# Leading products first in the block products and the down products, and the second block sum written over a weight block

## The chip, the cores and the metric

The kernel runs on one core of one Trainium2 chip. The metric is the device time of one execution in microseconds (us); the runs of the kernel before have a median of 2973.24 us (three runs, 2968.42 to 2973.53 us).

## The reference

What is computed is a decoder of two layers on 1024 tokens of width 1024, all in float32:

```python
for layer in range(DEPTH):                       # DEPTH = 2
    h = rmsnorm(x, norm_mix[layer])
    if layer < N_A_LAYERS:                       # layer 0: sparse attention, three gated branches
        mix = nsa_attention(h, a_w_in[i], ..., a_w_out[i], rel_bias)
    else:                                        # layer 1: shared keys and values, three dilated windows
        kv = (rmsnorm(x, kv_norm) @ kv_w).reshape(B, S, N_DIL, 2, N_KV, HEAD_DIM)
        mix = dilated_attention(h, b_w_q[j], k_shared, v_shared, b_w_out[j], rel_bias)
    x = x + mix
    x = x + swiglu(rmsnorm(x, norm_ffn[layer]), ffn_w_up[layer], ffn_w_down[layer])
return rmsnorm(x, final_norm)

def swiglu(h, w_up, w_down):
    a, b = jnp.split(h @ w_up, 2, axis=-1)       # w_up: 1024 x 5632, w_down: 2816 x 1024
    return (jax.nn.silu(a) * b) @ w_down
```

## The kernel before

**Products in three parts.** A float32 operand is split into a leading part h, rounded to the matmul's format on ScalarE (ACT), and a remainder l, a subtraction on VectorE (DVE). A product of two operands is then three matmuls: h by h, h by l, and l by h. `mm3` issues them in this order for one 128x128 piece of the stationary side, on its lines 203, 204 and 205. `Pairs` makes such a pair for a 128x512 operand: line 884 writes `ph` on ACT, line 885 writes `pl` on DVE (or, early in a stage, on GpSimd, POOL). There are five `ph` and five `pl` buffers, so a sixth pair waits until the first has been read by its last matmul.

**Block products.** The feed-forward up product, and the projection of keys, values and queries behind the first layer (`project_B`), are products of 2x2 blocks by the scheme of seven multiplications instead of eight. `cols_steps` does one block of 128 output columns: the weights come as four 128x512 blocks a11, a12, a21, a22 (`raw`, the tile names `oT` and `oTb` in the profile), and seven products m1 to m7 multiply a weight block, or a sum of blocks, by one of seven prepared operands of the token side, `B11`, `B21`, `B22` and `T1` to `T4`. `blk` issues a product: four pieces by three matmuls, 12 matmuls into one PSUM bank. POOL makes the sums: s1 = a21 + a22 (line 1112), a21 = a11 - a21 (line 1113), s2 = s1 - a11 (line 1127), a12 = a12 - s2 (line 1129). m5 multiplies s1 by T1, m6 multiplies s2 by T2, m7 a21 by T3, m4 a22 by T4, m3 a12 by B22. The banks: m1, m6, m7 and m4 accumulate in one bank after another (`ux`), which ACT copies out after m1 (line 1095), m6 (line 1134) and m7 (line 1143); m2 uses a bank that DVE empties on line 1104; m5 and m3 share one that DVE reads on lines 1144 and 1160.

**Down products.** Two hidden blocks of 128 columns make the operands of one call of `rows_steps`, again seven products of 12 matmuls: four row tiles t by three matmuls. Each row tile has a bank of its own, `dx0` to `dx3` for products that accumulate, `dr0` and `dr1` in turn for the others, and DVE adds a bank to the residual stream `xr` on line 943. Its sums run on POOL (lines 951 to 961).

**Order.** `staged` prepares a step (loads, sums, pairs) and then issues the matmuls of the step before. In `ffn`, two hidden blocks (14 block products) and the seven down products of the two blocks before are put in turn: two block products, one down product. A pair of hidden blocks is thus 252 matmuls. The order of a block's products is a string: in the feed-forward part "m1 m2 m5 m6 m7 m4 m3", in `project_B` "m1 m2 m6 m5 m7 m4 m3" for all but its first block. From these steps a scheduler works out, when the kernel is built, in which order each engine's instructions stand; on the chip each engine keeps that order. So matmuls of different steps are mixed where the scheduler took one to be ready before another.

**Loads.** Weight blocks of the feed-forward part turn through seven buffers (`wu`), those of `project_B` through ten; a load on SyncE's queue (SP) into a buffer waits for the last reader of what was in it. POOL multiplies each block by the norm's gains (lines 1269 and 1453). In the feed-forward part s2 is written over s1 (`s2=None`); in `project_B` it has a tile of its own.

Of the kernel before, what the change touches and what calls it, by code (L numbers as in the profile page):

```python
# [115 lines left out]
def trunk(ctx, tc, I, out):  # L116
    nc = tc.nc
# [83 lines left out]
    def mm3(ps, lhs, rhs, first, last, shared=False):  # L201
        (lh, ll), (rh, rl) = lhs, rhs
        nc.tensor.matmul(ps, lh, rh, start=first, stop=False, skip_group_check=bool(shared))  # L203
        nc.tensor.matmul(ps, lh, rl, start=False, stop=False, skip_group_check=bool(shared))  # L204
        return nc.tensor.matmul(ps, ll, rh, start=False, stop=last, skip_group_check=bool(shared))  # L205
# [189 lines left out]
    with ExitStack() as c:  # L395
# [145 lines left out]
        steps = compress(0, kc2, wts)  # L541
# [356 lines left out]
    def part(t, i):  # L898
        return t[0][:, i * 128:(i + 1) * 128], t[1][:, i * 128:(i + 1) * 128]
# [11 lines left out]
    def rows_steps(spare, pairs, tmp, blocks, xr):  # L911


        X, tA, tB = [], [], []
        n = len(blocks)

        def step(ops, onX, where, sums=None, whole=False, eng=(None, None)):
            def operands(i):
                if sums is not None:
                    sums(i, *blocks[i])  # L920
                return pairs(ops[0](i), eng[0]), pairs(ops[1](i), eng[1])

            def prep():
                ready = [operands(0)]

                def run():
                    if whole:
                        ready.extend(operands(i) for i in range(1, n))
                        order = [(i, t) for t in range(4) for i in range(n)]
                    else:  # L930
                        order = [(i, t) for i in range(n) for t in range(4)]
                    banks = X if onX else [bank(spare[t % len(spare)]) for t in range(4)]
                    if onX == 1:
                        X.extend(bank(f"dx{t}") for t in range(4))
                    for i, t in order:
                        if i == len(ready):
                            ready.append(operands(i))
                        a, b = ready[i]
                        mm3(banks[t], part(a, t), b, i == 0 and onX != 2, i == n - 1, onX)
                        if i == n - 1:  # L940
                            for r, c in where:
                                xs = xr[:, 4 * r + t, c * 512:(c + 1) * 512]
                                nc.vector.tensor_add(xs, xs, banks[t])  # L943
                return run
            return prep

        def sums1(i, a, b):
            (a11, a21, a12, a22), (b11, b12, b21, b22) = a, b
            tA.append(tmp("a", i))
            tB.append(tmp("b", i))  # L950
            nc.gpsimd.tensor_add(tA[i], a21, a22)
            nc.gpsimd.tensor_sub(tB[i], b12, b11)
            nc.gpsimd.tensor_sub(a21, a11, a21)
            nc.gpsimd.tensor_sub(b12, b22, b12)

        def sums2(i, a, b):
            (a11, a21, a12, a22), (b11, b12, b21, b22) = a, b
            nc.gpsimd.tensor_sub(tA[i], tA[i], a11)
            nc.gpsimd.tensor_sub(tB[i], b22, tB[i])
            nc.gpsimd.tensor_sub(a12, a12, tA[i])  # L960
            nc.gpsimd.tensor_sub(b21, b21, tB[i])

        P = nc.gpsimd if n > 1 else None
        A = lambda j: lambda i: blocks[i][0][j]
        B = lambda j: lambda i: blocks[i][1][j]
        T = lambda i: tA[i], lambda i: tB[i]
        return [step((A(0), B(0)), 1, [(0, 0)]),
                step((A(2), B(2)), 0, [(0, 0)]),
                step(T, 0, [(1, 1), (0, 1)], sums1),
                step(T, 2, [(0, 1)], sums2),  # L970
                step((A(2), B(3)), 0, [(0, 1)]),
                step((A(1), B(1)), 2, [(1, 1)], eng=(None, P)),
                step((A(3), B(2)), 2, [(1, 0)], whole=True, eng=(P, None))]
# [98 lines left out]
    def cols_steps(banks, order, pairs, tmp, ops, load, done, view=lambda x: x, eng=None):  # L1072
# [6 lines left out]
        held = lambda n, name: st.setdefault(n, bank(name)) if n not in st else st[n]  # L1079

        def blk(b, a, name, first, prev=None):
            for i in range(4):
                with after(prev if i == 0 else None):
                    mm = mm3(b, part(a, i), ops[name][i], first and i == 0, i == 3, True)
            return mm

        def m1():
# [34 lines left out]

        def m6():
            a11, a12, a21, a22 = st["W"]
            s = s1()
            s2 = tmp("s2") or s
            nc.gpsimd.tensor_sub(s2, s, a11)
            a = pairs(s2)
            nc.gpsimd.tensor_sub(a12, a12, s2)

            def run():
                blk(held("x", nx), a, "T2", False)
                st["d1"] = tmp("d1")
                nc.scalar.activation(st["d1"], view(st["x"][:]), AF.Copy)
            return run
# [116 lines left out]
    def ffn(p, scratch, B, xr, layer):  # L1252
# [1 line left out]
        pairs = Pairs(p, 5)  # L1254
        own = lambda n, bufs=1: p.tile([128, 512], F32, name=n, bufs=bufs)
        wu, ut = Turns(scratch[0:7]), Turns(scratch[7:13])
        misc = dict(c=scratch[13], s1=scratch[14], s2=None)
        wd = Turns([p.tile([128, 512], F32, name=f"wd{i}")[:] for i in range(3)] + scratch[15:])
        gains = g_ffn[layer]
        raw = {}  # L1260
# [19 lines left out]
        def hidden(j, u):  # L1280

            def ahead(f):
                if j == 1:
                    raw[2].clear()
                if 0 < j < NJ - 1:
                    for q in range(3):
                        load_up(j + 1, q)
                return f()

            def tmp(n):  # L1290
                if n in ("d0", "d1"):
                    return u[base + int(n[1])]
                return scratch[15] if (j, n) == (0, "c") else misc[n]

            def done(a, r, C):
                t = u[base + r]
                if a == 0:
                    nc.scalar.activation(t, C, AF.Silu)
                else:
                    nc.vector.tensor_mul(t, t, C)  # L1300

            base = 2 * (j % 2)
            banks = {0: ("dx2", "uy", "uy"), 1: ("dx3", "ux", "uy")}.get(j, ("ux", "uy", "uy"))
            steps = cols_steps(banks, "m1 m2 m5 m6 m7 m4 m3", pairs, tmp, B.ops, lambda: raw[j], done,
                               eng=nc.gpsimd if j < 3 else None)
            i = 2 if j in (1, 2) else 0
            steps[i] = steps[i][0], lambda f=steps[i][1]: ahead(f)

            def m4(f=steps[5][1]):
                if j == 0:  # L1310
                    raw[1].clear()
                if j + 1 < NJ:
                    for q in range(3 if j else 0, 4):
                        load_up(j + 1, q)
                return f()
            steps[5] = "m4", m4
            return steps
# [529 lines left out]
```

## Time and profile before

| | |
|---|---|
| median of the runs | 2973.24 us (2968.42 to 2973.53, three runs) |
| the profiled execution | 2975.66 us, its span 2973.8 us |
| mean granted TensorE clock | 0.989 |
| first attention stage | 0 to about 795 us |
| feed-forward part of layer 0 | about 795 to 1460 us |
| `project_B` | about 1460 to 1880 us |
| second attention stage | about 1880 to 2200 us |
| output projection and feed-forward part of layer 1 | about 2200 to 2960 us |

How to read the rows: PE is TensorE's matmuls, PEld its weight loads, DVE VectorE, ACT ScalarE, POOL GpSimd, SP SyncE. A name such as `ux<-T2h,ph` reads: into bank `ux`, moving operand the leading part of T2, stationary operand a `ph`. In the order of time, each row has the start, the duration, the engine, the line, the operation, and in brackets how long the engine sat idle before it and who released it. A matmul's duration there is longer than the distance to the next one, since matmuls overlap; so a short wait of the matmuls shows as a longer distance between two starts, and not in brackets.

### The profile page before, as it was taken

How to read it: one execution, taken by the hardware profiler on the slowest of the kernel's cores; microseconds unless marked ns; L12 is line 12 of the kernel's file. 1: busy time of each engine (PE TensorE's matmuls, PEld its weight loads, DVE VectorE, ACT ScalarE, POOL GpSimd, SP SyncE). 2: the span in 40 equal slices, each digit the busy share in tenths (PEclk: the TensorE clock that was granted, in tenths of full speed). 3: DMA queues.
4: the chain of work that ended last, by engine and by line, in shares of the span. 5: the costliest groups of instructions: out<-in, count | busy, mean ns of one | idle time of the engine just before them, and what ended most of it. 6: DMA issues, size and time to landing. Idle time of an engine off the chain costs nothing.

```text
span 2973.8 us, 44470 instructions
## 1 busy us (share of the span) xinstructions
PE 2842.3 (96%) x14734; PEld 2372.2 (80%) x14734; DVE 2394.0 (81%) x4866; ACT 1610.0 (54%) x3615; POOL 1616.4 (54%) x1727
## 2 busy tenths in 40 slices
PE   9999999999999999999999999899989999999997
PEld 8888888887777788788777788788867788887886
DVE  5543988988988888988875676699998888888887
ACT  5432988897553333333454444699965433333334
POOL 2135766764565555555456787444425755555552
PEclk9999999999999999999999999999999999999999
DMA  8678133113222222231224554865441211112112
GB/s 242 219 241 289 43 95 87 50 34 112 73 62 63 74 74 62 63 77 56 85 82 130 164 170 145 264 207 175 126 153 32 68 57 57 57 47 63 51 47 75
DMA packets 277318, 317.58 MB, mean 107 GB/s; under 512 B 19196, under 2 KB 210733, under 8 KB 277088
## 3 DMA queue, kind: packets, MB, share of 16 engines
q1 hardware_dynamic: 255344, 246.50, 28.0%
q0 software_dynamic: 21744, 68.23, 7.1%
q8 instruction: 117, 1.92, 0.3%
q14 instruction: 113, 0.93, 0.1%
HBM read 243.17 MB, written 87.20 MB: 111 GB/s over the span
## 4 chain that ended last, share of the span: by engine, by line
PE 60%; DVE 23%; ACT 6%; issue 4%; DMA 3%; POOL 3%; SPq 1%; DVEq 0%; POOLq 0%; ACTq 0%
PE ux L203 5%; DVE pl L885 5%; PE ux L204 5%; PE ux L205 5%; PE uy L203 4%; PE uy L204 4%; PE uy L205 4%; DVE xr L943 4%; PE dx L204 3%; PE dx L205 3%; PE pt L328 3%; PE dr L203 3%; PE dx L203 2%; PE mm L204 2%; PE dr L204 2%
## 5 line engine op out<-in xcount | busy, mean ns | idle before, releaser
L885 DVE TENSOR_TENSOR pl<-oT,ph 128x512 fp32r<-128x512 f32 x319 | 327.0, 1044 | 44.4 <-ACT ph L884 38.4
L884 ACT ACTIVATE ph<-oT 128x512 fp32r<-128x512 f32 x329 | 198.6, 625 | 208.6 <-PE ux L204 58.2
L328 PE MATMUL pt<-ident,P 128*128 128x128 f32 x1536 | 243.1, 276 | 11.2 <-DVE tl L166 5.1
L885 DVE TENSOR_TENSOR pl<-oTb,ph 128x512 fp32r<-128x512 f32 x233 | 219.5, 967 | 25.1 <-ACT ph L884 25.0
L166 DVE TENSOR_TENSOR tl<-pt,th 128x512 fp32r<-128x512 f32 (+1 forms) x336 | 217.6, 653 | 27.0 <-ACT th L165 25.6
L884 ACT ACTIVATE ph<-oTb 128x512 fp32r<-128x512 f32 x239 | 142.8, 625 | 168.6 <-PE ux L204 52.4
L943 DVE TENSOR_TENSOR xr<-xr,dr 128x512 f32<-128x512 f32 x320 | 204.4, 678 | 30.0 <-PE dr L205 30.0
L204 PE MATMUL dx<-pl,ph 128*128 128x512 f32 x512 | 205.8, 402 | 9.6 <-DVE pl L885 7.0
L165 ACT ACTIVATE th<-pt 128x512 fp32r<-128x512 f32 (+1 forms) x336 | 185.1, 564 | 40.2 <-PE pt L328 35.7
L803 POOL TENSOR_SCALAR P<-P,sm,gates 128x384 f32<-128x384 f32 (+7 forms) x256 | 182.4, 723 | 44.9 <-DVE sm L801 39.7
L328 PEld LDWEIGHTS pt<-ident,P 128*128 128x128 f32 x1536 | 178.4, 141 | 31.9 <-DVE tl L166 5.2
L943 DVE TENSOR_TENSOR xr<-xr,dx 128x512 f32<-128x512 f32 x320 | 200.0, 678 | 2.5 <-PE dx L205 1.8
L205 PE MATMUL dx<-ph,pl 128*128 128x512 f32 x512 | 201.4, 396 | 0.4 <-DVE pl L885 0.4
L203 PE MATMUL dx<-ph 128*128 128x512 f32 x512 | 164.6, 401 | 14.5 <-DVE nss L1016 7.9
L799 ACT ACTIVATE P<-P,m 128x384 f32<-128x384 f32 (+7 forms) x256 | 170.6, 669 | 9.2 <-DVE m L797 7.1
L1269 POOL TENSOR_TENSOR oT<-oT,gffn 128x512 f32<-128x512 f32 x92 | 108.8, 1188 | 121.9 <-DMA oT<-in_ffn_w_up_dram 98.5
L348 PE MATMUL o<-th,V 128*128 128x256 f32 x572 | 159.0, 297 | 5.1 <-POOL th L341 2.0
L349 PE MATMUL o<-tl,V 128*128 128x256 f32 x572 | 158.2, 299 | 3.2 <-DVE tl L166 1.5
L1269 POOL TENSOR_TENSOR oTb<-oTb,gffn 128x512 f32<-128x512 f32 x92 | 108.2, 1186 | 89.3 <-DMA oTb<-in_ffn_w_up_dram 74.4
L341 POOL TENSOR_SCALAR th<-traw 128x256 fp32r<-128x256 f32 x112 | 95.4, 852 | 101.9 <-ACT traw L340 37.1
L1646 ACT ACTIVATE P<-P,st 128x384 f32<-128x384 f32 (+2 forms) x256 | 139.8, 548 | 6.7 <-DVE st L1641 5.3
L203 PEld LDWEIGHTS dx<-ph 128*128 128x128 f32 x512 | 96.9, 190 | 43.9 <-ACT nss L1015 8.7
(631 smaller groups left out, 9502.6 us busy)
## 6 DMA issues: line engine op xcount, KB each, us to landing
qB<-xr POOLq DMA_DIRECT2D x96, 256.0 KB, 4.6
oT<-in_ffn_w_up_dram SPq DMA_DIRECT2D x92, 256.0 KB, 2.9
oTb<-in_ffn_w_up_dram SPq DMA_DIRECT2D x92, 256.0 KB, 3.0
Q<-qB SPq DMA_DIRECT2D x40, 512.0 KB, 5.9
wd<-in_ffn_w_down_dram SPq DMA_DIRECT2D x66, 256.0 KB, 2.6
oT<-in_b_w_q_dram SPq DMA_DIRECT2D x48, 256.0 KB, 4.2
K<-kBs SPq DMA_DIRECT2D x40, 256.0 KB, 9.9
wraw<-in_a_w_in_dram SPq DMA_DIRECT2D x18, 512.0 KB, 7.8
```

The source lines that it names most:

```text
L165: prev = nc.scalar.activation(H_, src, AF.Copy)
L166: rest = (eng or nc.vector).tensor_sub(L_, src, f32(H_))
L203: nc.tensor.matmul(ps, lh, rh, start=first, stop=False, skip_group_check=bool(shared))
L204: nc.tensor.matmul(ps, lh, rl, start=False, stop=False, skip_group_check=bool(shared))
L205: return nc.tensor.matmul(ps, ll, rh, start=False, stop=last, skip_group_check=bool(shared))
L328: nc.tensor.transpose(ps[:, i * 128:(i + 1) * 128], b, ident)
L799: nc.scalar.activation(P[:, e, :n], P[:, e, :n], AF.Exp, bias=mm[:, e:e + 1], scale=-1.0, accum_out=sm[:, e:e + 1])
L803: nc.gpsimd.tensor_scalar(P[:, e, :n], P[:, e, :n], sm[:, e:e + 1], gt(g, t, br, 2 * hp + e, 1), op0=OP.mult, op1=OP.mult)
L884: nc.scalar.activation(h, src, AF.Copy)
L885: (eng or nc.vector).tensor_sub(l, src, f32(h))
L943: nc.vector.tensor_add(xs, xs, banks[t])
L1269: nc.gpsimd.tensor_mul(v, v, gains[:, k:k + 4].unsqueeze(2).to_broadcast([128, 4, 128]))
```

## The change

Three things change. First, `blk` issues the twelve matmuls of a block product by kind: the four leading products (prepared h by weight h), then the four with the prepared operand's remainder, then the four with the weight pair's remainder `pl`. Second, `rows_steps` issues a down product by pairs of row tiles, 0 and 1, then 2 and 3, and within a pair by kind: leading, then the remainder of the left (stationary) operand, then that of the right one. Third, s2 is written over a11 and not over s1 or into a tile of its own, and the feed-forward part uses the order "m1 m2 m6 m5 m7 m4 m3" for all blocks but the first. The number of instructions on each engine stays as it is.

```diff
@@ rows_steps
...
-                    for i, t in order:
-                        if i == len(ready):
-                            ready.append(operands(i))
-                        a, b = ready[i]
-                        mm3(banks[t], part(a, t), b, i == 0 and onX != 2, i == n - 1, onX)
-                        if i == n - 1:
+                    (a, b), = ready
+                    for ts in ((0, 1), (2, 3)):
+                        for z, (u, v) in enumerate(((0, 0), (1, 0), (0, 1))):
+                            for t in ts:
+                                nc.tensor.matmul(banks[t], part(a, t)[u], b[v], start=z == 0 and onX != 2, stop=z == 2,
+                                                 skip_group_check=True)
+                        for t in ts:
                             for r, c in where:
                                 xs = xr[:, 4 * r + t, c * 512:(c + 1) * 512]
                                 nc.vector.tensor_add(xs, xs, banks[t])
@@ cols_steps, blk
-            for i in range(4):
-                with after(prev if i == 0 else None):
-                    mm = mm3(b, part(a, i), ops[name][i], first and i == 0, i == 3, True)
+            (ah, al), oh, ol = a, [o[0] for o in ops[name]], [o[1] for o in ops[name]]
+            for z, (x, ys) in enumerate(((ah, oh), (ah, ol), (al, oh))):
+                for i in range(4):
+                    with after(prev if (z, i) == (0, 0) else None):
+                        mm = nc.tensor.matmul(b, x[:, i * 128:(i + 1) * 128], ys[i], start=first and (z, i) == (0, 0),
+                                              stop=(z, i) == (2, 3), skip_group_check=True)
@@ cols_steps, m6
-            s = s1()
-            s2 = tmp("s2") or s
-            nc.gpsimd.tensor_sub(s2, s, a11)
-            a = pairs(s2)
-            nc.gpsimd.tensor_sub(a12, a12, s2)
+            nc.gpsimd.tensor_sub(a11, s1(), a11)
+            a = pairs(a11)
+            nc.gpsimd.tensor_sub(a12, a12, a11)
@@ ffn
-            steps = cols_steps(banks, "m1 m2 m5 m6 m7 m4 m3", pairs, tmp, B.ops, lambda: raw[j], done,
+            steps = cols_steps(banks, "m1 m2 m6 m5 m7 m4 m3" if j else "m1 m2 m5 m6 m7 m4 m3", pairs, tmp, B.ops, lambda: raw[j], done,
```

The changed kernel is three lines shorter from line 941 on: lines 1112, 1127 and 1129 of before are 1111, 1124 and 1126 there, block products stand on line 1082, down products on 934.

**Place 1**, PE in the middle of the feed-forward part: the product m6 (T2) and the leading matmuls of the down product beside it. Before, T2's pair is `ph_13783`, `pl_13784`, and `pl_13766` belongs to the down product's right operand:

```order
L205 MATMUL uy_13746<-B21h3_10177,pl_13721 128x512
L203 MATMUL dx0_13510<-ph_13765,ph_13761 128x512
L203 MATMUL dx1_13511<-ph_13765,ph_13761 128x512
L203 MATMUL ux_13706<-T2h0_11010,ph_13783 128x512
L204 MATMUL ux_13706<-T2l0_11011,ph_13783 128x512
L203 MATMUL dx2_13512<-ph_13765,ph_13761 128x512
L203 MATMUL dx3_13513<-ph_13765,ph_13761 128x512
L204 MATMUL dx0_13510<-pl_13766,ph_13761 128x512
L205 MATMUL dx0_13510<-ph_13765,pl_13762 128x512
```

Now T2's pair is `ph_13743`, `pl_13744`, made before the down product's two pairs:

```order
L1082 MATMUL uy_13748<-B21h3_10177,pl_13721 128x512
L1082 MATMUL ux_13706<-T2h0_11010,ph_13743 128x512
L1082 MATMUL ux_13706<-T2h1_11012,ph_13743 128x512
L1082 MATMUL ux_13706<-T2h2_11014,ph_13743 128x512
L1082 MATMUL ux_13706<-T2h3_11016,ph_13743 128x512
L1082 MATMUL ux_13706<-T2l0_11011,ph_13743 128x512
L1082 MATMUL ux_13706<-T2l1_11013,ph_13743 128x512
L1082 MATMUL ux_13706<-T2l2_11015,ph_13743 128x512
L1082 MATMUL ux_13706<-T2l3_11017,ph_13743 128x512
L934 MATMUL dx0_13512<-ph_13767,ph_13763 128x512
L1082 MATMUL ux_13706<-T2h0_11010,pl_13744 128x512
```

T2's first eight matmuls moved ahead of the down product, whose first matmul stands eight places later.

**Place 2**, PE a little further on in the same block: from T3 (m7) to T4 (m4), which accumulate in the same bank. Before:

```order
L205 MATMUL ux_13706<-T3h3_11024,pl_13805 128x512
L204 MATMUL dr0_13849<-pl_13826,ph_13821 128x512
L205 MATMUL dr0_13849<-ph_13825,pl_13822 128x512
L204 MATMUL dr1_13850<-pl_13826,ph_13821 128x512
L205 MATMUL dr1_13850<-ph_13825,pl_13822 128x512
L203 MATMUL ux_13706<-T4h0_11026,ph_13845 128x512
```

And now:

```order
L1082 MATMUL ux_13706<-T3h3_11024,pl_13805 128x512
L934 MATMUL dr0_13849<-ph_13825,ph_13821 128x512
L934 MATMUL dr1_13850<-ph_13825,ph_13821 128x512
L934 MATMUL dr0_13849<-ph_13825,pl_13822 128x512
L934 MATMUL dr1_13850<-ph_13825,pl_13822 128x512
L934 MATMUL dr0_13849<-pl_13826,ph_13821 128x512
L934 MATMUL dr1_13850<-pl_13826,ph_13821 128x512
L1082 MATMUL ux_13706<-T4h0_11026,ph_13845 128x512
```

Six matmuls of the down product stand between T3 and T4 where four stood.

**Place 3**, POOL in the same block. Before, after the last sum of a down product:

```order
L961 TENSOR_TENSOR wd2_11044<-wd2_11044,tb_13615 128x512
L1269 TENSOR_TENSOR oT_2663<-oT_2663,gffn0_734 128x512
L1127 TENSOR_TENSOR oT_2663<-oT_2663 128x512
L1129 TENSOR_TENSOR oT_2663<-oT_2663 128x512
L1269 TENSOR_TENSOR oT_2663<-oT_2663,gffn0_734 128x512
```

And now:

```order
L957 TENSOR_TENSOR wd2_11044<-wd2_11044,tb_13615 128x512
L1124 TENSOR_TENSOR oT_2663<-oT_2663 128x512
L1266 TENSOR_TENSOR oT_2663<-oT_2663,gffn0_734 128x512
L1126 TENSOR_TENSOR oT_2663<-oT_2663 128x512
L1266 TENSOR_TENSOR oT_2663<-oT_2663,gffn0_734 128x512
```

The second block sum stands one place earlier and is written over a11.

**Place 4**, PE in the last block of `project_B`: from T2 (m6, bank `ux`) to T1 (m5), with a second half of B21 (m2, bank `dr0`) around it. T1 goes into bank `dr1`, which m5 and m3 share, and which DVE empties on line 1160 (1157 of the changed kernel) after m3 of the block before. Before:

```order
L205 MATMUL ux_19365<-T2h3_16605,pl_19431 128x512
L203 MATMUL dr0_19536<-B21h0_10171,ph_19514 128x512
L204 MATMUL dr0_19536<-B21l0_10172,ph_19514 128x512
L203 MATMUL dr1_19482<-T1h0_16591,ph_19460 128x512
L204 MATMUL dr1_19482<-T1l0_16592,ph_19460 128x512
```

And now:

```order
L1082 MATMUL ux_19349<-T2h3_16605,pl_19414 128x512
L1082 MATMUL dr0_19519<-B21h0_10171,ph_19497 128x512
L1082 MATMUL dr0_19519<-B21h1_10173,ph_19497 128x512
L1082 MATMUL dr0_19519<-B21h2_10175,ph_19497 128x512
L1082 MATMUL dr0_19519<-B21h3_10177,ph_19497 128x512
L1082 MATMUL dr0_19519<-B21l0_10172,ph_19497 128x512
L1082 MATMUL dr0_19519<-B21l1_10174,ph_19497 128x512
L1082 MATMUL dr0_19519<-B21l2_10176,ph_19497 128x512
L1082 MATMUL dr0_19519<-B21l3_10178,ph_19497 128x512
L1082 MATMUL dr1_19465<-T1h0_16591,ph_19443 128x512
```

Eight matmuls of B21 stand between T2 and T1 where two stood.

More of the change, by code (lines that the diff above doesn't have):

```diff
@@ L926, in run @@
                 def run():
[L927 to L931, printed above, removed]
                     banks = X if onX else [bank(spare[t % len(spare)]) for t in range(4)]
@@ L1256, in ffn @@
         wu, ut = Turns(scratch[0:7]), Turns(scratch[7:13])
-        misc = dict(c=scratch[13], s1=scratch[14], s2=None)
+        misc = dict(c=scratch[13], s1=scratch[14])
         wd = Turns([p.tile([128, 512], F32, name=f"wd{i}")[:] for i in range(3)] + scratch[15:])
```

## The prediction

> **What bounds the kernel now.** I read the head of the page first: the span and the busy time of each engine.
>
> ```profile
> span 2973.8 us, 44470 instructions
> PE 2842.3 (96%) x14734; PEld 2372.2 (80%) x14734; DVE 2394.0 (81%) x4866; ACT 1610.0 (54%) x3615; POOL 1616.4 (54%) x1727
> ```
>
> PE is busy 96% of the span and no matmul is removed, so an edit of order can win only the distance between the matmuls' sum and the span in the stages it touches. These stages I read from the table of windows (length and end, PE's busy time and number of matmuls, then PEld, DVE, ACT, POOL, granted clock, DMA):
>
> ```profile
> 900.00:1460.00 560.00, 556.94 (x2411) 449.94 (x2410) 491.70 (x669) 213.10 (x369) 305.08 (x228) 1.00 0.26 67
> 1700.00:1880.00 180.00, 177.77 (x780) 145.73 (x779) 118.85 (x127) 82.93 (x129) 126.99 (x139) 1.00 0.57 171
> 2400.00:2960.00 560.00, 556.13 (x2410) 449.63 (x2408) 482.84 (x675) 220.14 (x392) 292.55 (x222) 1.00 0.18 55
> ```
>
> Busy time hides short waits, since matmuls overlap. So I take the pitch from the rows of PE in order of time, which also show one pair of hidden blocks at the places of the change:
>
> ```profile
> 1084.41 0.61 PE L203 MATMUL dx<-ph 128*128 128x512 f32 x2
> 1085.04 0.50 PE L203 MATMUL ux<-T2h,ph 128*128 128x512 f32 x1
> 1085.37 0.39 PE L204 MATMUL ux<-T2l,ph 128*128 128x512 f32 x1
> 1085.61 0.63 PE L203 MATMUL dx<-ph 128*128 128x512 f32 x2
> 1086.30 0.51 PE L204 MATMUL dx<-pl,ph 128*128 128x512 f32 x1
> 1086.64 0.40 PE L205 MATMUL dx<-ph,pl 128*128 128x512 f32 x1
> ...
> 1090.52 0.39 PE L203 MATMUL uy<-T1h,ph 128*128 128x512 f32 x1
> ...
> 1093.24 0.62 PE L203 MATMUL dr<-ph 128*128 128x512 f32 x2
> ...
> 1097.10 0.39 PE L205 MATMUL dr<-ph,pl 128*128 128x512 f32 x1
> 1097.56 0.50 PE L203 MATMUL ux<-T4h,ph 128*128 128x512 f32 x1
> 1097.90 0.40 PE L204 MATMUL ux<-T4l,ph 128*128 128x512 f32 x1
> ```
>
> The twelve matmuls of T1 run undisturbed: (1093.24 - 1090.52)/12 = 0.2267 us each. At that pitch 2411 matmuls take 546.6 us of the first window's 560 and 2410 take 546.3 of the last's: 13.4 and 13.7 us lost. A pair of hidden blocks is 252 x 0.2267 = 57.1 us, so the two windows hold 2 x 560/58.5 = 19.2 pairs (58.5 with its waits), and each loses 27.1/19.2 = 1.4 us.
>
> The same rows show where. T2 should start two pitches after the first row, at 1084.86; it starts at 1085.04 and its second matmul stands 0.33 behind instead of 0.23: 0.18 + 0.10 = 0.28 us. `dx<-pl`, the down product's right remainder, should start at 1086.06 and starts at 1086.30, the next 0.34 behind: 0.24 + 0.11 = 0.35. T4 should start at 1097.33 and starts at 1097.56, the next 0.34 behind: 0.34. Together 0.97 us of the pair's 1.4.
>
> **Why these three wait.** The rows of the other engines at these times:
>
> ```profile
> 1081.88 1.29 DVE L885 TENSOR_TENSOR pl<-oT,ph 128x512 fp32r<-128x512 f32 x2
> 1083.08 2.47 DVE L943 TENSOR_TENSOR xr<-xr,dx 128x512 f32<-128x512 f32 x4
> 1085.47 0.77 DVE L885 TENSOR_TENSOR pl<-wd,ph 128x512 fp32r<-128x512 f32 x1
> ...
> 1082.64 1.68 POOL L1127 TENSOR_TENSOR oT<-oT 128x512 f32<-128x512 f32 x1 [7.15 <-DVE pl L885]
> ...
> 1084.35 1.15 ACT L884 ACTIVATE ph<-oT 128x512 fp32r<-128x512 f32 x2 [2.00 <-PE uy L204]
> ...
> 1096.39 0.63 ACT L884 ACTIVATE ph<-oT 128x512 fp32r<-128x512 f32 x1 [2.48 <-PE ux L204]
> 1096.93 0.58 ACT L1143 ACTIVATE oT<-ux 128x512 f32<-128x512 f32 x1
> ```
>
> T2: POOL's sum s2 overwrites s1, so it waits 7.15 us for DVE to make s1's `pl`, ends at 1084.32, and ACT makes T2's leading part only then. `dx<-pl`: DVE adds four banks to `xr` and makes the right remainder after them, done at 1086.24. T4: it accumulates in the bank that ACT copies out after T3; that copy stands on ACT behind a `ph` which waited 2.48 us for a buffer that T3's eleventh matmul (L204) gave back, and ends at 1097.51.
>
> **The change part by part.** *s2 over a11, T2 before T1 (feed-forward).* The same instructions issue on every engine; no DMA is added. The sum needs only s1, which POOL itself made, and a11, whose last reader is m1's pair long before; its 7.15 us wait is gone. T2 is asked for eight places earlier (8 x 0.2267 = 1.81 us), but its pair also stands ahead of the down product's two, so neither DVE's remainder nor POOL sets its time. I take its wait as gone.
>
> *Leading products first.* In a block product the weight's `pl` is needed after eight matmuls instead of two, 6 x 0.2267 = 1.36 us later, and the `ph` buffer is free after eight instead of eleven, 3 x 0.2267 = 0.68 us earlier. For T4 that takes the `ph` off ACT ahead of the copy (1096.39 - 0.68 = 1095.71, before T3 ends), so the copy runs at T3's end, and six fillers instead of four give it 0.45 us more against a wait of 0.23: gone. In the down product the right remainder comes last: at place 1 eleven other matmuls stand between the first leading one and it, so it is asked for 12 x 0.2267 = 2.72 us after the down product starts, and that start itself is eight places later: about 1084.41 + 1.81 + 2.72 = 1088.9, against its 1086.24. Gone.
>
> These three are 0.97 x 19.2 = 18.6 us if every pair were like this one. The bound above is all 27.1; below, nothing may be won if the waits go elsewhere. I take six sevenths, 16 us, since each has slack left by the rows; the 0.43 us a pair that I don't name stays.
>
> *`project_B`.* The waits of PE there, and the last of the first kind in order of time; the third line is from the start of the feed-forward part:
>
> ```profile
> PE dr L203 <- DVE d L1160: 3.9, 5, 1.9
> PE uy L203 <- ACT c L1143: 0.7, 1, 0.7
> ...
> 1792.61 0.39 PE L204 MATMUL dr<-B21l,ph 128*128 128x512 f32 x1
> 1794.10 0.50 PE L203 MATMUL dr<-T1h,ph 128*128 128x512 f32 x1 [1.11 <-DVE d L1160]
> ...
> PE dx L203 <- ACT oT L1134: 0.6, 1, 0.6
> ```
>
> T1 waits for the bank that m3 of the block before used. Eight matmuls of B21 stand ahead of it now, not two, so it asks 1.36 us later. Of five waits of 3.9 us together the longest is 1.9 and keeps about 0.5; the others go: -3.4. The 0.7 us wait for L1143 loses two fillers' 0.45. Sum -3.9. In the window 1700:1880 that cannot be too much: 780 x 0.2267 = 176.8 leaves 3.2 us lost there, and the rest of the waits lies before 1700.
>
> *Second hidden block of each layer.* T3 waits 0.6 us for T2's copy (L1134); T1's twelve matmuls now stand between, so it goes: -0.6, and as much in layer 1 by the same order, -1.2.
>
> *The long wait in `project_B`.* In POOL's order one of two gain products moves behind six stores, so the sum L1129 no longer waits for its load:
>
> ```profile
> 1610.05 1.04 POOL L1453 TENSOR_TENSOR oT<-oT,gmix 128x512 f32<-128x512 f32 x1 [2.09 <-DMA oT<-in_b_w_q_dram]
> ...
> 1612.74 3.15 POOL L1510 DMA_DIRECT2D vBs<-oT  x6
> ...
> 1617.06 0.30 PE L1503 MATMUL dx<-ident,d 128*128 128x128 f32 x1 [3.79 <-DVE oT L166]
> ...
> 1619.07 0.63 PE L205 MATMUL ux<-T3h,pl 128*128 128x512 f32 x1
> ...
> 1624.18 0.40 PE L205 MATMUL uy<-B11h,pl 128*128 128x512 f32 x1
> ```
>
> PE waits 3.79 us behind this row of POOL, and then runs 12 matmuls in 5.11 us, 0.426 each: the slow clock costs some 13 x 0.2 = 2.6 us more. If the load is no longer in the way, all 6.4 us go; if the moved product (1.04 us) or the six stores (3.15) come in front of it, the wait grows by as much. Either end is open; I take 0 and keep -6.4 and +4.2. By the Trainium skill ("TensorE: Matmul & The Clock Gate", Part 1) the clock halves after an idle window of about 3.4 us; the trace agrees in this place (0.426 after 3.79 us of waiting). By it, a wait cut by 0.4 would already save the 2.6 too, and the sum be 3.0 lower, 2951.6 instead of 2954.6.
>
> **Sum.** -16 - 3.9 - 1.2 + 0 = -21.1 us. From the profiled execution's 2975.66 that is 2954.6; the runs' median (2973.24) stands 2.4 below it, so I predict 2952 us. A difference of 0.2% (6 us) is about what a measurement of this kernel can tell from none.
>
> **Rivals.** *The waits only move.* The down product asks for its left remainder after two matmuls, where it came after five: 3 x 0.2267 = 0.68 us earlier. If two of the seven down steps of a pair now wait 0.45 us, two thirds of that, it is 0.9 x 19.2 = 17 us, and -21 + 17 = -4 is left: about 2969. For it: DVE is 491.70/560 = 88% busy there and in strict order. Against it: the left pair is made first, and the rows above show the right one as the late one. Chance 0.17.
>
> *Slower: POOL's sums on top of DVE's remainders.* These rows are groups of the window 900:1460, then two DVE rows of the pair above:
>
> ```profile
> L885 DVE TENSOR_TENSOR pl<-oT,ph 128x512 fp32r<-128x512 f32 x192 | 191.1, 1022 | 17.8 <-ACT ph L884 17.8
> L943 DVE TENSOR_TENSOR xr<-xr,dx 128x512 f32<-128x512 f32 x155 | 96.7, 677 | 1.1 <-PE dx L205 0.9
> L1127 POOL TENSOR_TENSOR oT<-oT 128x512 f32<-128x512 f32 x19 | 28.0, 1473 | 80.8 <-DVE pl L885 80.8
> ...
> 1086.17 0.68 DVE L885 TENSOR_TENSOR pl<-oT,ph 128x512 fp32r<-128x512 f32 x1
> ...
> 1090.36 5.50 DVE L885 TENSOR_TENSOR pl<-oT,ph 128x512 fp32r<-128x512 f32 x4
> ```
>
> A remainder takes 0.68 us alone, 1.02 on the mean, and four took 5.50 while POOL summed without a pause; the additions to `xr`, with one operand in PSUM, stay at 0.677. The wait of the sum for `pl` kept the two apart; without it the sum runs beside remainders. If one sum a pair holds up a remainder on PE's path by its own 1.47 us, that is 1.47 x 19.2 = 28, and 28 - 21 = +7: about 2973 + 7 = 2980. It decides from 21/19.2 = 1.1 us a pair on. Against it: in block products a late remainder has 1.36 us more room. Chance 0.09. The Trainium skill ("SBUF — State Buffer", section "SBUF: two separate sides") states the mechanism: DVE with two SBUF operands and GpSimd share a port pair as an exclusive lock, held for a whole instruction. The rows of this kernel agree (0.68 against 1.02 and 5.50/4).
>
> *More than named.* If the unnamed 0.43 us a pair go too (8.3 us) and the long wait of `project_B` with them (6.4), -36: about 2937. For it: later remainders help every product, not only the three. Chance 0.12.
>
> **How the numbers follow.** The forecast, between -12 and -32 us, has 0.62. The range 2936 to 2970 takes in the forecast, most of the larger gain and the waits that move; the slower rival is left out. Faster by over 0.2%: the forecast, the larger gain and a little of the first rival, 0.76; within 0.2%: 0.15; slower: 0.09.
>
> **What would show it.** In the changed kernel POOL's s2 no longer waits for DVE; T2, T4 and the right remainder start at the pitch behind their neighbours; the loss in the two feed-forward windows falls from 27 us to about 11; T1's wait for line 1157 in `project_B` is near 0.5 us. Wrong would be new distances above 0.23 us at `dx<-ph,pl` (left remainder), or DVE's mean remainder well above 1.02 us.

## The result and the profile after

The changed kernel takes 2939.94 us (median of four runs, 2930.58 to 2941.60) against 2970.83 us of the kernel before on the same chips: a ratio of 0.9888, 95% interval 0.9868 to 0.9908. It is 31 us faster; 2952 was forecast. The profiled execution took 2938.84 us. That of the kernel before took 2975.66 us, 4.8 us above the median of its runs, so falls measured against its windows may come out some 5 us too large in all. The head of the changed kernel's page (span, then busy time of each engine):

```profile
span 2937.1 us, 44584 instructions
PE 2816.6 (96%) x14734; PEld 2375.5 (81%) x14734; DVE 2398.0 (82%) x4866; ACT 1621.1 (55%) x3615; POOL 1642.7 (56%) x1727
```

The counts of the five engines are those of before.

To see where 36.7 us of span went, one cuts both executions at the same matmuls, counted from the start: a window from the 4901st to the 7481st matmul (feed-forward part of layer 0, with its start), one from the 7701st to the 9341st (most of `project_B`), one from the 12241st to the 14501st (steady feed-forward part of layer 1). The table of windows of the kernel before, and then of the changed one (length, PE, PEld, DVE, ACT, POOL busy with counts, granted clock, DMA):

```profile
832.88:1432.15 599.27, 590.64 (x2581) 476.31 (x2580) 522.52 (x703) 233.26 (x405) 340.33 (x253) 1.00 0.25 67
1488.09:1878.30 390.21, 371.23 (x1641) 301.57 (x1640) 258.26 (x306) 184.32 (x304) 261.57 (x282) 0.97 0.47 142
2379.99:2902.49 522.50, 520.47 (x2261) 422.46 (x2260) 453.19 (x624) 197.32 (x340) 289.20 (x214) 1.00 0.18 54
```

```profile
830.12:1413.24 583.12, 579.64 (x2581) 478.61 (x2580) 516.68 (x702) 235.07 (x401) 357.60 (x254) 1.00 0.25 69
1470.81:1851.98 381.17, 366.40 (x1641) 298.35 (x1640) 274.14 (x304) 185.25 (x306) 254.66 (x280) 0.99 0.50 146
2351.90:2864.17 512.27, 512.27 (x2261) 424.17 (x2260) 446.63 (x627) 203.07 (x341) 304.31 (x215) 1.00 0.18 55
```

The lengths fall by 16.2, 9.0 and 10.2 us, 35.4 together; the four stretches between and around them change by 1.6 to 2.8 us each, two of them up. In the third window 2260 matmuls at the pitch of 0.2267 us are 512.3 us: nothing is lost there any more, where 10.2 us were lost before.

The rows of PE at the place that the prediction shows (same pair of hidden blocks), and below them the rows of POOL, DVE and ACT that decide there:

```profile
1072.81 1.07 PE L1082 MATMUL uy<-B21h,pl 128*128 128x512 f32 x4
1073.71 1.07 PE L1082 MATMUL ux<-T2h,ph 128*128 128x512 f32 x4
...
1078.02 0.39 PE L934 MATMUL dx<-ph,pl 128*128 128x512 f32 x1
1078.24 1.07 PE L934 MATMUL dx<-pl,ph 128*128 128x512 f32 x4
...
1085.50 0.61 PE L934 MATMUL dr<-pl,ph 128*128 128x512 f32 x2
1085.95 1.07 PE L1082 MATMUL ux<-T4h,ph 128*128 128x512 f32 x4
...
1064.87 1.29 POOL L1124 TENSOR_TENSOR oT<-oT 128x512 f32<-128x512 f32 x1
...
1074.85 0.69 DVE L885 TENSOR_TENSOR pl<-wd,ph 128x512 fp32r<-128x512 f32 x1
...
1084.79 0.60 ACT L1140 ACTIVATE oT<-ux 128x512 f32<-128x512 f32 x1 [0.27 <-PE ux L1082]
```

Each start follows the one before at the pitch (four matmuls are 0.907 us, 1072.81 to 1073.71). The sum s2 (L1124) has no bracket, so it waited for nobody; it starts 8.8 us ahead of T2's first matmul, where before it ended 0.7 us ahead. The right remainder is done at 1075.54 and asked for at 1078.24. ACT's copy ends at 1085.39, T4 starts at 1085.95. That s2 hardly waits for DVE any more holds for the window 900:1410 as a whole, where the prediction's row has 80.8 us in 19 times:

```profile
L1124 POOL TENSOR_TENSOR oT<-oT 128x512 f32<-128x512 f32 x18 | 26.9, 1493 | 5.7 <-DVE pl L885 5.7
```

In `project_B` the waits changed their names. PE's waits there (total, times, longest), first of the kernel before beside those that the prediction shows, then of the changed one in the second window:

```profile
PE dx L1503 <- DVE oT L166: 4.2, 2, 3.8
...
PE ux L203 <- ACT d L1134: 1.9, 2, 1.3
...
PE uy L203 <- ACT d L1134: 1.4, 2, 0.7
```

```profile
PE ux L1082 <- ACT d L1131: 4.7, 4, 1.8
...
PE uy L1082 <- ACT d L1131: 2.0, 3, 0.9
PE dx L1500 <- DVE oT L166: 1.8, 2, 1.2
...
PE dr L1082 <- DVE d L1157: 0.2, 1, 0.2
```

T1's waits for its bank (L1160 before, now L1157) fell from 3.9 to 0.2 us, the transposes' from 4.2 to 1.8; but T3 now waits 4.7 + 2.0 = 6.7 us for the copy after T2 (L1131, which was L1134), where it waited 3.3. That is taken up by the fourth experiment.

### The profile page after: what moved, and what is told of

Read it like the earlier page. It is cut to its first block, busy times and chain, and to the rows that moved or that the text cites. A ratio compares the mean times of both kernels' runs of the same rounds, so it can differ in the third digit from the quotient of the medians.

```text
span 2937.1 us, 44584 instructions
## 1 busy us (share of the span) xinstructions
PE 2816.6 (96%) x14734; PEld 2375.5 (81%) x14734; DVE 2398.0 (82%) x4866; ACT 1621.1 (55%) x3615; POOL 1642.7 (56%) x1727
## 5 line engine op out<-in xcount | busy, mean ns | idle before, releaser
L885 DVE TENSOR_TENSOR pl<-oT,ph 128x512 fp32r<-128x512 f32 x337 | 350.8, 1058 | 57.5 <-PE dr L934 17.4
L884 ACT ACTIVATE ph<-oT 128x512 fp32r<-128x512 f32 x347 | 210.9, 626 | 203.7 <-PE ux L1082 54.6
L885 DVE TENSOR_TENSOR pl<-oTb,ph 128x512 fp32r<-128x512 f32 x233 | 213.2, 937 | 28.9 <-PE dr L934 17.4
L1638 DVE CUSTOM_DVE_ANT_0 P<-s,T 128x384 f32<-128x384 f32 (+2 forms) x256 | 114.8, 476 | 12.8 <-PE s L1677 4.6
L349 PEld LDWEIGHTS o<-tl,V 128*128 128x128 f32 x572 | 108.6, 190 | 16.5 <-DVE tl L166 11.0
L348 PEld LDWEIGHTS o<-th,V 128*128 128x128 f32 x572 | 108.9, 190 | 12.4 <-DVE o L360 5.3
L884 ACT ACTIVATE ph<-wd 128x512 fp32r<-128x512 f32 x86 | 53.6, 627 | 99.8 <-PE ux L1082 48.5
```

The costliest lines, as they stand in the source:

```text
L348: nc.tensor.matmul(o_, v, th[:, cs], start=first, stop=False, skip_group_check=True)
L349: return nc.tensor.matmul(o_, v, tl[:, cs], start=False, stop=last, skip_group_check=True)
L884: nc.scalar.activation(h, src, AF.Copy)
L885: (eng or nc.vector).tensor_sub(l, src, f32(h))
```

## The experiments

Three theories stood after the result. The prediction's: each part removes its own waits. Rival A, later sharpened to C: the part on s2 does nearly all in the feed-forward parts. Rival B: the order in the block product does. Each ratio is against the kernel before on the same chip.

**1, block order alone.** The kernel before, with this edit only:

```diff
-            for i in range(4):
-                with after(prev if i == 0 else None):
-                    mm = mm3(b, part(a, i), ops[name][i], first and i == 0, i == 3, True)
+            for z, (x, ys) in enumerate(((ah, oh), (ah, ol), (al, oh))):
+                for i in range(4):
...
```

> Only the order within a block product is changed (leading, prepared remainder, weight remainder); down products, s2 and the order of m5 and m6 stay as before. Theory of the prediction (each edit removes its own waits): the waits at T4 (5.5 us over both feed-forward parts) and at the right remainder of the down product (5.2) go, T2's 6.4 stay, T1's waits in project_B shrink by 3: about -13 us, 2958. Rival A (s2 over a11 with m6 first does nearly all): -5 or less, 2966 or more. Rival B (the block order does nearly all): -25 to -30, 2943.

Measured: 2958.93 us, ratio 0.9965 (0.9953 to 0.9977), -12 us: the size that the first theory gave, but not at its place. The first and third windows are 592.42 and 520.55 us, `project_B` 379.81: falls of 6.9, 2.0 and 10.4 us, in a profile whose span is 16.7 us below that of before. So the most lies in `project_B`, where about 3 was expected, and only 2 in the steady feed-forward part. There T4 does start on time, behind six matmuls of the down product, and so does the right remainder at place 1. But there is a new wait (PE row, then DVE):

```profile
2430.21 0.39 PE L203 MATMUL dx<-ph 128*128 128x512 f32 x1
2431.40 0.50 PE L203 MATMUL dx<-ph 128*128 128x512 f32 x1 [0.81 <-DVE xr L943]
...
2429.34 1.41 DVE L885 TENSOR_TENSOR pl<-oTb,ph 128x512 fp32r<-128x512 f32 x1
2430.67 1.27 DVE L943 TENSOR_TENSOR xr<-xr,dx 128x512 f32<-128x512 f32 x2
```

The down product's leading matmuls come before T2 and need a bank that DVE has not yet added to `xr`, because a remainder stands ahead of the addition. This row is one of the two longest; in most pairs its start is 0.27 us late. The right remainder of a `dr` product, further on, is late too (0.2 us in most pairs). Summed over the window, starts later than the pitch cost 8.3 us here and 10.2 before.

**2, down order alone.** The kernel before, with the edit of `rows_steps` only:

```diff
-                        mm3(banks[t], part(a, t), b, i == 0 and onX != 2, i == n - 1, onX)
...
+                    for ts in ((0, 1), (2, 3)):
+                        for z, (u, v) in enumerate(((0, 0), (1, 0), (0, 1))):
...
```

> Only the order within a down product is changed (two row tiles at a time, by kind). Theory of the prediction: the right remainder's 5.2 us in the two feed-forward parts go and nothing else: -5 us, 2966. Rivals A and B: within 2 us of before, since the down order without the others only moves the wait to the left remainder.

Measured: 2964.54 us, 0.9983 (0.9971 to 0.9994), -5 us by the ratio, the number that the first theory gave, but not for its reason. The third window is 519.92 us. The right remainder, whose wait was to go, still waits there (it is due at 2439.94), and T4 as before; what went is most of T2's wait and of that of the leading matmuls:

```profile
2439.71 0.40 PE L934 MATMUL dx<-ph,pl 128*128 128x512 f32 x1
2440.17 0.96 PE L934 MATMUL dx<-pl,ph 128*128 128x512 f32 x3
...
2450.27 0.61 PE L934 MATMUL dr<-pl,ph 128*128 128x512 f32 x2
2450.96 0.50 PE L203 MATMUL ux<-T4h,ph 128*128 128x512 f32 x1
```

T4 should start at 2450.72 and is 0.24 late; four matmuls stand between T3 and T4 in this order. `project_B`, which has no down products, is 5.1 us shorter in the profile; the edit itself does not explain that. 4.7 us of it are PE's busy time there (366.54 us against 371.23): the profile of before has more matmuls at the slow pace.

**3, the part on s2 alone.**

```diff
-            s2 = tmp("s2") or s
-            nc.gpsimd.tensor_sub(s2, s, a11)
-            a = pairs(s2)
-            nc.gpsimd.tensor_sub(a12, a12, s2)
+            nc.gpsimd.tensor_sub(a11, s1(), a11)
+            a = pairs(a11)
+            nc.gpsimd.tensor_sub(a12, a12, a11)
...
-"m1 m2 m5 m6 m7 m4 m3"
+"m1 m2 m6 m5 m7 m4 m3" if j else "m1 m2 m5 m6 m7 m4 m3"
```

> Only the sum and the order of products are changed: s2 is written over a11 everywhere, and the feed-forward part issues m6 before m5; block and down products keep their three matmuls a piece. Theory of the prediction: T2's 6.4 us go, the others stay or partly go: -6 to -9 us, about 2963. Rival A: the feed-forward waits go nearly whole, since in this order too six matmuls stand between T3 and T4 and twelve of T2 ahead of the down product: -20 to -25 us, 2948. Rival B: within 3 us of before.

Measured: 2953.49 us, 0.9941 (0.9929 to 0.9953), -17.5 us. The third window:

```profile
2364.27:2877.55 513.28, 512.99 (x2261) 424.04 (x2260) 473.22 (x624) 196.86 (x340) 293.17 (x215) 1.00 0.18 54
```

9.2 of the 10.2 us of that window go with this part alone, T4's and the right remainder's waits among them (one of 0.45 us is left), though no order within a product is changed. Rival A holds for the steady part; in the first window (591.17) half is left, nearly all of it at its start: from the 4901st to the 5185th matmul are 69.83 us here, 62.69 in the changed kernel.

**4, two buffers for d1.** The changed kernel; in `project_B` the tile that s2 no longer needs takes every second copy of the bank after T2.

```diff
-                t = own(name + str(n % 2) if name == "d0" else name)
+                t = own(name + str(n % 2) if name == "d0" else "s2" if name == "d1" and n % 2 else name)
```

> The changed kernel, and in project_B the copy of the bank after T2 (d1) goes into two buffers in turn, the second one the tile that s2 no longer needs. In the changed kernel T3 waits there 6.7 us in all (7 waits) for that copy, which waits for the block before to have split its d1. If that is what holds the copy: these waits go, -4 to -7 us against the changed kernel, about 2934 (base 2971). If ACT's strict order holds it behind something else: within 2 us of the changed kernel, 2940.

Measured: 2923.76 us, 0.9842 (0.9830 to 0.9855): 47 us below before, by the ratios 14 below the changed kernel, twice the most that was expected. The chain in the changed kernel, in DVE, ACT and PE:

```profile
1667.78 2.98 DVE L885 TENSOR_TENSOR pl<-oT,ph 128x512 fp32r<-128x512 f32 x1
1670.69 1.83 DVE L170 SCALAR_TENSOR_TENSOR xr<-d,xr 128x512 fp32r<-128x512 f32 x1
...
1672.61 0.60 ACT L1131 ACTIVATE d<-ux 128x512 f32<-128x512 f32 x1 [3.01 <-DVE xr L170]
...
1673.26 0.96 PE L1082 MATMUL ux<-T3h,ph 128*128 128x512 f32 x3 [1.49 <-ACT d L1131]
```

The copy waits until DVE has split the d1 of the block before, DVE is held up by a remainder, and T3 waits for the copy. With two buffers the same copy has no bracket, and T3 follows B21 at the pitch:

```profile
1664.68 0.59 ACT L1131 ACTIVATE d<-ux 128x512 f32<-128x512 f32 x1
...
1666.35 0.62 PE L1082 MATMUL dr<-B21h,pl 128*128 128x512 f32 x2
1666.81 0.39 PE L1082 MATMUL ux<-T3h,ph 128*128 128x512 f32 x1
```

The second window falls from 381.17 to 364.05 us. That is more than the 6.7 us of waits for the copy: the listed waits of PE in the window fall from 14.8 to 3.6 us, the 1.8 at the transposes among them, and PE's busy time falls from 366.40 to 360.17 us, with the granted clock up from 0.99 to 1.00. Not all of that is the edit's: seven slow matmuls of the changed kernel (from 1478.93 us) stand ahead of its first wait for d1.

**5, 6 and 7, one part undone.** The changed kernel with the old block order, with the old down order, and without the part on s2 (the hunks above, reversed).

> The changed kernel with the block products back in the old order of their twelve matmuls (three a piece); down order and s2 over a11 with m6 first are kept. Theory of the prediction (the late weight remainder and the early free ph take T4's wait and most of the rest): 12 us lost, about 2952 at a base of 2971. Theory C, formed on the runs before (any order with T2 ahead of the down product and six matmuls between T3 and T4 removes these waits, whatever the order within a product): the feed-forward parts stay as in the changed kernel, 3 to 8 us lost in project_B and single waits, 2943 to 2948.

> The changed kernel with the down products back in the old order; block order and s2 over a11 with m6 first are kept. Theory of the prediction: the right remainder's wait (5 us) comes back in part, 2943 to 2945. Theory C: the same as the changed kernel, 2940, since T2's products stand ahead of the down product and give its remainders time.

> The changed kernel without the part on s2 (s2 over s1 and m5 first in the feed-forward part, a tile of its own in project_B); block and down order are kept. If the parts add up: the 12 and the 6.5 us of the two parts alone, 2953. Theory C: six matmuls stand between T3 and T4 here too, so T4 is free; the down product's leading matmuls stand ahead of T2 again and wait for the banks that DVE adds to xr: 2950 to 2955, with 5 us or more of waits of dx for xr.

Measured, with the lengths of the three windows (us). The windows are those of one profiled execution each, the ratios those of all runs; where the two disagree, the ratio counts:

| kernel | time | ratio (95%) | layer 0 | project_B | layer 1 |
|---|---|---|---|---|---|
| before | | | 599.27 | 390.21 | 522.50 |
| 1, block alone | 2958.93 | 0.9965 (0.9953-0.9977) | 592.42 | 379.81 | 520.55 |
| 2, down alone | 2964.54 | 0.9983 (0.9971-0.9994) | 596.12 | 385.14 | 519.92 |
| 3, s2 alone | 2953.49 | 0.9941 (0.9929-0.9953) | 591.17 | 377.45 | 513.28 |
| 7, block and down | 2964.97 | 0.9982 (0.9970-0.9994) | 593.00 | 380.80 | 523.06 |
| 5, down and s2 | 2942.33 | 0.9899 (0.9876-0.9922) | 587.71 | 386.48 | 512.62 |
| 6, block and s2 | 2937.90 | 0.9884 (0.9866-0.9903) | 584.61 | 376.48 | 513.14 |
| all (changed kernel) | 2939.94 | 0.9888 (0.9868-0.9908) | 583.12 | 381.17 | 512.27 |

The fifth and the sixth kernel came near what theory C said (2943 to 2948, and 2940), not what the first theory did (2952, and 2943 to 2945). The seventh missed both: without the part on s2 the other two are worth 5 us, less than the block order alone (12), where 2950 to 2955 us were expected. In layer 1 nothing is won against before. T4 is on time, as theory C had it, but the waits are not those for `xr` that it named:

```profile
2440.08 0.61 PE L934 MATMUL dr<-ph,pl 128*128 128x512 f32 x2
2441.01 0.73 PE L934 MATMUL dr<-pl,ph 128*128 128x512 f32 x2 [0.31 <-DVE pl L885]
...
2489.29 1.07 PE L934 MATMUL dx<-ph 128*128 128x512 f32 x3
2490.59 0.98 PE L934 MATMUL dx<-ph,pl 128*128 128x512 f32 x3 [0.23 <-DVE pl L885]
```

Two down steps a pair wait for a remainder. The one, for the right remainder of a `dr` product, starts at 2441.01 and was due at 2440.53 (0.48 us, and much the same in each pair); the other, for the left remainder of a `dx` product, at 2490.59 and was due at 2489.97 (0.62; but in five of the eight pairs that show it, it is 0.12 to 0.16 late). With the longer distances right behind them they cost 7.7 us in the window, 0.86 a pair. That is near the 0.9 of the rival "the waits only move", but the left remainder, the one that it named, has the smaller share (3.05 us). Both need the down product ahead of T2. With s2 in a11 and m6 ahead of m5 the steady part is free whichever order the products have (512.27 to 513.28 in four kernels of the table). The down order can't be told from nothing next to the other two (0.9884 against 0.9888); the old block order beside them costs at most a little (0.9899). Added to the part on s2 alone, though, the down order wins (0.9899 against 0.9941, intervals apart, 12 us). The windows place only 3.5 and 0.7 us of that, and `project_B` is longer; where it comes from is not shown.

**8, s2 over a11, but m5 first.** The changed kernel with the old string in the feed-forward part:

```diff
-"m1 m2 m6 m5 m7 m4 m3" if j else "m1 m2 m5 m6 m7 m4 m3"
+"m1 m2 m5 m6 m7 m4 m3"
```

> The changed kernel, but m5 stands ahead of m6 in the feed-forward part again; s2 is still written over a11. If the place of s2 is what counts (its sum no longer waits for DVE's remainder of s1): as the changed kernel within 3 us, 2940. If the order of the products counts (T2's pair ahead of the down product's pairs): most of the 14 us that the block and down order alone lack come back, 2948 to 2953.

Measured: 2950.03 us, 0.9928 (0.9909 to 0.9948), in the range given for the order. The place of s2 and the order each hold a part: the third window is 518.71, between 523.06 (neither) and 512.27 (both). What is left is mostly T4, 4.1 of the 6.4 us over the changed kernel (PE's rows, then ACT's):

```profile
2437.32 0.39 PE L1082 MATMUL ux<-T3h,pl 128*128 128x512 f32 x1
2437.54 0.61 PE L934 MATMUL dr<-pl,ph 128*128 128x512 f32 x2
2438.39 1.19 PE L1082 MATMUL ux<-T4h,ph 128*128 128x512 f32 x4 [0.24 <-ACT oTb L1140]
...
2436.83 0.63 ACT L884 ACTIVATE ph<-oTb 128x512 fp32r<-128x512 f32 x1 [2.93 <-PE ux L1082]
2437.74 0.60 ACT L1140 ACTIVATE oTb<-ux 128x512 f32<-128x512 f32 x1 [0.27 <-PE ux L1082]
```

Here two matmuls stand between T3 and T4, and T4 is 0.40 late (2437.99 was due). From T3's last start to T4's are 1.07 us; before, with the old block order, 1097.56 - 1096.19 = 1.37. The `ph` is off ACT at 2437.46, and the copy waits for T3's end alone. So the earlier free `ph` brings the copy forward, by 0.30 us, as the prediction reckoned, but six matmuls (7 x 0.2267 = 1.59 us from start to start) cover either. The number of fillers, the matmuls that stand between T3 and T4, decides. Each pair has two T4s. In the steady part, its first pair apart, one of them has four fillers in the kernel before and in the second, two in this one; in all other kernels both have six.

**9 and 10, with two d1 buffers.** The fourth kernel with the old down order; and the part on s2 alone with two buffers.

> The kernel with two d1 buffers, with the down products back in the old order. If the down order is worth nothing once T2 stands ahead of the down product: 2922 to 2926, as with it. If its worth was hidden behind the d1 waits of project_B (no down product is there, so this should not be): 2928 or more.

> Only the part on s2, with two d1 buffers in project_B; block and down products in the old order. Theory C: the block order is worth nothing in the steady feed-forward part and pays in project_B alone. The s2 part alone has 2953; its waits for d1 there are 2.9 us, so -4 to -8: 2945 to 2949, and 20 us or more are missing to the kernel with all parts and two d1 buffers. If d1's buffer alone makes the difference in project_B, whatever the block order: 2930.

Measured: 2929.02 us, 0.9856 (0.9835 to 0.9877), and 2942.58, 0.9906 (0.9889 to 0.9922). The first time lies in the range of the second reading (2928 or more), but it can't be told from the fourth kernel (0.9830 to 0.9855): beside the other two parts the down order is still not shown to be worth anything. The second came better than its 2945 to 2949, but 19 us behind the fourth. The ninth and the tenth differ in the block order alone: 584.01, 366.00 and 513.14 us against 590.99, 371.20 and 512.61. So the block order pays 7.0 us in layer 0's part, nearly all at its start (62.69 against 68.99 us from the 4901st to the 5185th matmul), 5.2 in `project_B` and nothing in the steady part. The fourth kernel has the lowest ratio of all.

## Why the prediction was right, and where not

*Direction and size.* Faster was right, and 2940 lies in the range, nearer to "more than named" (2937) than to 2952. Both mechanisms named in that rival came true: in the steady part the unnamed loss went too, and so did the long wait.

*The feed-forward parts* were forecast at -16, so that of 27 us some 11 would stay lost. Cut at the matmuls of the prediction's own two windows (2409 in each), the lengths fall from 559.58 to 548.55 and from 558.63 to 550.76 us, 18.9 together; against the pitch 7.7 us stay lost, where 26.6 were. So the term had nearly the right size. It held back in the steady part, where all waits went, not six sevenths of the named ones; but the matmuls from the 14501st to the last of layer 1 take 1.6 us more than before (57.76 against 56.13). The first table has -26.4 mainly because its first window begins earlier: 4.5 us were won from the 4901st to the 5185th matmul (67.19 to 62.69), where the prediction had one wait of 0.6.

*Who removes them.* This step failed. The prediction let each part remove its own waits, and credited T4 and the right remainder to the order within the products. The block order alone does set T4 and one right remainder free, but other waits come in their place (8.3 of 10.2 us stay lost); the third experiment removes all of them but one in the steady part, without any change of order within a product, and the seventh, which has both orders, leaves the steady part as it was. The parts alone were to give about 13, 5 and 6 to 9 us; they gave 12, 5 and 17.5, the first two largely by other waits than named, so that their agreement is luck. What counts is that T2's pair, no longer tied to DVE's remainder of s1, lets T2's matmuls stand ahead of the down product; these give the down product's remainders their time, and the scheduler then puts six fillers ahead of T4. By its sentence on slack (1088.9 for the right remainder) the prediction had the effect in hand, but put it under the wrong edit.

*`project_B`.* -3.9 was forecast, -9.0 is in the window, 4.8 of it in PE's busy time (371.23 to 366.40 us), which the slow matmuls make longer. T1's term was right (3.9 to 0.2 us; about 0.5 was to stay). The -0.45 for the copy on L1143, now L1140, did not come: that wait is 0.7 us before and after. The long wait, taken at 0 between -6.4 and +4.2, went to the lower end: 0.65 us are left, and no slow matmuls behind it. POOL's and PE's rows of the changed kernel:

```profile
1587.10 1.62 POOL L1126 TENSOR_TENSOR oT<-oT 128x512 f32<-128x512 f32 x1
1588.67 3.17 POOL L1507 DMA_DIRECT2D vBs<-oT  x6
...
1592.87 0.33 PE L1500 MATMUL dx<-ident,d 128*128 128x128 f32 x1 [0.65 <-DVE oT L166]
...
1594.12 1.20 PE L1082 MATMUL ux<-T3h,ph 128*128 128x512 f32 x4 [0.82 <-ACT d L1131]
```

The gain product that had waited for its load ahead of the sum now stands behind the six stores (at 1591.84), as the prediction had it. Four matmuls then take 1.20 us, so the pace is fast. The Trainium skill ("TensorE: Matmul & The Clock Gate", Part 1), by which an idle window of about 3.4 us halves the clock, agrees with this place. Another place differs from it, and there the measurement decides: in the kernel before seven matmuls take 0.43 us each (1573.33 to 1576.31 us) after waits of 0.38 and 1.30 us, and in the second kernel, with waits of 0.27 and 1.15 us at the same place, none does. So the length of one wait does not settle it; what does is not shown. Against these gains the waits of T3 for d1 grew from 3.3 to 6.7 us, which was not forecast; the fourth experiment shows their price, 14 us with what hangs on them.

*The second hidden block* (-1.2) was right: both waits of 0.6 us for T2's copy are gone from PE's list in the changed kernel, and in the first, while the third still has them. So the block order removes them, as forecast.

*The slower rival.* Page rows of DVE's remainders, before and then after:

```profile
L885 DVE TENSOR_TENSOR pl<-oT,ph 128x512 fp32r<-128x512 f32 x319 | 327.0, 1044 | 44.4 <-ACT ph L884 38.4
L885 DVE TENSOR_TENSOR pl<-oTb,ph 128x512 fp32r<-128x512 f32 x233 | 219.5, 967 | 25.1 <-ACT ph L884 25.0
```

```profile
L885 DVE TENSOR_TENSOR pl<-oT,ph 128x512 fp32r<-128x512 f32 x337 | 350.8, 1058 | 57.5 <-PE dr L934 17.4
L885 DVE TENSOR_TENSOR pl<-oTb,ph 128x512 fp32r<-128x512 f32 x233 | 213.2, 937 | 28.9 <-PE dr L934 17.4
```

546.5/552 = 0.990 us before, 564.0/570 = 0.989 after: on the mean a remainder costs what it did. In the first of the prediction's windows, cut at the same matmuls, the group that it named went from 1.02 to 1.04 us, which is not well above. The collision that the Trainium skill names ("SBUF — State Buffer", section "SBUF: two separate sides") is still there, in the 2.98 us of one remainder above, during which POOL ran without a pause, and in `project_B` it had reached PE's path by way of d1.

*Left open.* The first attention stage, whose code is the same, was 3 us shorter in the profile after, the second 2 us longer; windows of single profiles that differ by such amounts, as `project_B` between the fifth and the sixth kernel in part, are not explained here. A measure of that scatter: in the twelve profiles the last matmul of the first stage on lines 328 to 349 starts between 723.7 and 730.3 us. The waits at the start of layer 0's part in the third and tenth kernels were not traced to their cause.

## What to carry to other kernels

Where a build-time scheduler orders the work, price an edit by the order that it leads to, and test the parts in all their pairs: here two edits that each won alone won less together than the better one alone, until the third gave the scheduler another product to put ahead. A sum that overwrites its own input ties an engine to the reader of that input; write it over a block that has been read long ago. After each gain read the list of waits again for a buffer that has become the tight one, and see whether the edit has freed a tile for it.

## What the runs showed of the hardware

Nothing that contradicts the profile before. One number is new: in the steady part of layer 1, 2260 matmuls of 128x512 took 512.26 to 512.27 us, 0.2267 each with no gap, while DVE was busy 446.63/512.27 = 87% and POOL 59% of it; so at this load of the other engines the pitch itself does not suffer.
